# An FFN's output GEMM by seven block products for 16 of 22 f-tiles, its input GEMM in two passes, and the weight sums on GpSimd

## The chip, the cores and the metric

The kernel runs on one core of a Trainium2 chip. The metric is the device time of one execution in microseconds (us); lower is better. The engines are the tensor engine (PE, whose weight loads are shown as PEld), the vector engine (DVE), the scalar engine (ACT), GpSimd (POOL) and the sync engine (SP, which here only issues DMAs). Each works through its own queue in order, and semaphores hold them together.

## The reference

One encoder block on x of 1024 tokens by 1024 features in float32:

```python
def swiglu(x, w_in, w_out):
    gate, up = jnp.split(x @ w_in, 2, axis=-1)
    return (jax.nn.silu(gate) * up) @ w_out

x = x + 0.5 * swiglu(rmsnorm(x, ffn1_norm_g), ffn1_w_in, ffn1_w_out)   # D_FF = 2816
proj = rmsnorm(x, mix_norm_g) @ w_mix_in        # 8200 columns: mLSTM, spatial gating, gates
x = x + (sigmoid(g_m) * h_m + sigmoid(g_s) * h_s) @ w_mix_out
x = x + 0.5 * swiglu(rmsnorm(x, ffn2_norm_g), ffn2_w_in, ffn2_w_out)
return rmsnorm(x, final_norm_g)
```

The change touches the two FFNs only. Between them lies the mixing stage, which keeps its code.

## The kernel before

**Layout and precision.** Activations lie with features on the 128 partitions and 512 tokens (one of two token halves) in the free dimension. A float32 operand is used as a high part in float32r and the float32r remainder; a product of two operands is three matmuls (high-high, high-low, low-high: `PROD`). `unit` makes such a pair from a weight tile: a cast on ACT and a subtraction on DVE (L286, L287); `split` (L190, L191) does the same for an activation.

**Input GEMM.** w_in has 22 f-tiles of 128 gate columns and 22 of 128 up columns. For one f-tile, the features (two halves of 512), the tokens (two halves) and the pair gate/up form a 2 x 2 by 2 x 2 block product, and `group` computes it with seven block products in place of eight (the Winograd form of Strassen's scheme). Each product is 4 k tiles x 3 = 12 matmuls of 128 x 128 by 512 columns (`prod`, L293). The weight operands are sums and differences of the four raw blocks (`combine`, L299, on DVE); the activation operands, `B["t1"]` to `B["t4"]` and `B["22"]`, are made once by `operands`. Two of the seven products, with `B["11"]` and `B["21"]`, need only the first token half. For the first ten f-tiles (`EARLY`) `first_products` computes these two ahead of time, while the second token half is still being turned, and sends the results (`eb`) to DRAM; `group` fetches them back through POOL's DMA queue (L331, L333). For the other twelve f-tiles `group` does all seven. A group ends with the two h tiles of its f-tile, gate and up already multiplied and split. It is a generator: its first half ends at the `yield` of L346, its second after both h tiles.

**Output GEMM.** The f-tiles form blocks of three (the last has four, `BLOCKS`, L21). When a block's groups are done, its `down` is held back until the first half of the next block's first group has been issued. `down` takes w_out in four loads, and for each of eight output tiles and both token halves runs n x 3 matmuls (`down_mm`, L394), scales by 0.5 on ACT (L386) and adds into the residual in DRAM with an accumulating DMA from POOL (L387). The last block goes through `last`, which adds into the loaded residual (L421) and calls what follows.

**Buffers and order.** Raw weights have 3 buffers for the whole program (`rawp`), split weights 4 (`fw`), weight sums 3 (`fs`), h and early tiles 8 (`hp`), FFN temporaries 6 (`cp`, tag c) and general temporaries 4. Six PSUM banks serve the products. `bigp`, 16 tiles, holds `B["11"]`, `B["21"]`, `B["22"]` and `B["t4"]` during an FFN. The framework puts each engine's instructions in an order of its own; the program's order gives the priority. SP issues the weight loads, POOL the eb traffic and the accumulates.

Of the kernel before, what the change touches and what calls it, by code (L numbers as in the profile page):

```python
# [13 lines left out]
P = 128  # L14
# [6 lines left out]
BLOCKS = [(0, 3), (3, 3), (6, 3), (9, 3), (12, 3), (15, 3), (18, 4)]  # L21
EARLY = 10
SPAD = 40
MPAD = 24
HEADS = 4
# [8 lines left out]
def block_body(ctx, tc, x, ffn1_norm_g, ffn1_w_in, ffn1_w_out, mix_norm_g, w_mix_in, mlstm_conv_w,  # L34
# [8 lines left out]
    rawp = ctx.enter_context(tc.tile_pool(name="rawp", bufs=3))  # L43
    bigp = ctx.enter_context(tc.tile_pool(name="bigp", bufs=16))
    tps = []
    sp = ctx.enter_context(tc.tile_pool(name="sp", bufs=2))
# [14 lines left out]
    def open_temps(stack, n, bufs):  # L61
        tps.append(stack.enter_context(tc.tile_pool(name=f"tp{n}", bufs=bufs, reuse_waits="tile")))

    open_temps(f1, 1, 4)
# [53 lines left out]
    eb = [[[tc.dram_tile([P, NH], F32, name=f"eb{s}{f}{j}") for j in range(2)] for f in range(EARLY)]  # L118
          for s in range(2)]

    def load_unit(w_rows, ks, c0, extra=None):
        n = len(ks)
        nc_ = 2 * P if extra is None else 2 * P + extra[1]
        raw = rawp.tile([P, n, nc_], F32, tag="raw", name="raw")
# [138 lines left out]
    class Ffn:  # L263
        def __init__(self, stack, n, w_in, w_out):
            pool = lambda nm, b: stack.enter_context(tc.tile_pool(name=nm + n, bufs=b, reuse_waits="tile"))
            self.tx = pool("tx", 12)
            self.hp, self.wp, self.sp_ = pool("hp", 8), pool("fw", 4), pool("fs", 3)
            self.cp = pool("cp", 6)
            self.w_in, self.w_out = w_in, w_out
            self.B = {}  # L270
            self.eb = eb[int(n) - 1]

        def c512(self):
            return self.cp.tile([P, NH], F32, tag="c", name="c")

        def raw(self, f, d, both):
            r = rawp.tile([P, 4, 2, P], F32, tag="raw", name="raw")
# [12 lines left out]
        def prod(self, bank, w, b, start, stop):  # L290
            for i in range(4):
                for pi, (x, y) in enumerate(PROD):
                    PE.matmul(out=bank, lhsT=w[:, x, i, :], rhs=self.B[b][i][:, y, :],  # L293
                              start=(start and i == 0 and pi == 0), stop=(stop and i == 3 and pi == 2),
                              skip_group_check=True)

        def combine(self, a, b, op):
            s = self.sp_.tile([P, 4, P], F32, tag="s", name="s")
            V.tensor_tensor(out=s, in0=a, in1=b, op=op)  # L299
            return s  # L300

        def first_products(self, fs):
            st = []
            for f in fs:
                w = self.unit(self.raw(f, 0, False)[:, :, 0, :])
                a = bank("mm")
                self.prod(a, w, "11", True, False)
# [4 lines left out]
            for f, a, e in st:  # L312
                w = self.unit(self.raw(f, 1, False)[:, :, 0, :])
                self.prod(a, w, "21", False, True)
# [3 lines left out]
        def group(self, f):  # L318
# [3 lines left out]
            early = f < EARLY  # L322
            if not early:
                w = self.unit(a11)
                a = bank("mm")
                self.prod(a, w, "11", True, False)
                p1 = self.c512()
                A.copy(out=p1, in_=a)
            else:
                p1 = self.c512()  # L330
                G.dma_start(out=p1, in_=self.eb[f][0])  # L331
                sg1 = self.c512()
                G.dma_start(out=sg1, in_=self.eb[f][1])  # L333
            s1 = self.combine(a21, a22, ALU.add)
            s2 = self.combine(s1, a11, ALU.subtract)
            w = self.unit(s2)
# [4 lines left out]
            if not early:  # L341
                w = self.unit(a12)
                self.prod(a, w, "21", False, True)
                sg1 = self.c512()
                A.activation(out=sg1, in_=a, func=AF.Silu)
            yield  # L346
            s3 = self.combine(a11, a21, ALU.subtract)
            w = self.unit(s3)
            b = bank("mm")
            self.prod(b, w, "t3", True, True)  # L350
# [4 lines left out]
            self.prod(d, w, "t1", True, False)  # L355
# [652 lines left out]
```

## Time and profile before

| what | value |
|---|---|
| median of three runs | 2301.2 us (2300.08 to 2303.76) |
| the profiled execution | 2302.14 us, span 2300.0 us |
| PE busy | 2263.1 us (98%), 11171 matmuls |
| DVE busy | 1355.5 us (59%) |
| ACT busy | 992.9 us (43%) |
| POOL busy | 270.1 us (12%), nearly all of it issuing DMAs |
| DMA | 282.08 MB, mean 123 GB/s |

The stages by PE's timeline: the start and the first products of FFN1 to about 95 us, FFN1's groups and blocks to 699, the mixing stage to 1615, FFN2 to 2300. Busy is the share of time in which an engine executes; its idle time is put down to the instruction that released it last. Matmul ends are modelled, so the period of a run of matmuls is read from the starts of two neighbouring runs.

### The profile page before, as it was taken

The numbers are of one execution on the slowest core, as the hardware profiler recorded it, in microseconds if no ns is written. First come the engines' busy times: TensorE is split into PE (matmuls) and PEld (weight loads), VectorE is DVE, ScalarE is ACT, GpSimd is POOL, SyncE is SP. The second block draws the span as 40 slices with busy tenths as digits, with TensorE's granted clock in tenths as the row PEclk, the third lists the DMA queues.
The fourth block names the chain that finished last, engine by engine and source line by source line (L and its number), as shares of the span: only waits on it lengthen the run. The fifth ranks groups of instructions, "written<-read, shape, count | busy, mean of one in ns | idle before, by whom it ended". The sixth has DMA issues, their size and how long they took to land. (4 is left out here: it accounts for less than half of the span.)

```text
span 2300.0 us, 29669 instructions
## 1 busy us (share of the span) xinstructions
PE 2263.1 (98%) x11171; PEld 1908.0 (83%) x11171; DVE 1355.5 (59%) x2409; ACT 992.9 (43%) x1589; POOL 270.1 (12%) x394
## 2 busy tenths in 40 slices
PE   7999999999999999999999999999999999999998
PEld 5788888888888988888889888888778888888887
DVE  6845644634666658556646575565775446446466
ACT  5533333333345346445434554543633333333332
POOL 2221121021020000000000000000312220210200
PEclk9999999999999999999999999999999999999999
DMA  8775575274453234322353353324757772643633
GB/s 259 226 150 131 140 130 101 69 133 88 96 180 114 83 92 120 98 86 83 92 152 97 92 156 92 92 74 133 244 151 158 143 141 69 129 97 79 124 101 110
DMA packets 280367, 282.08 MB, mean 123 GB/s; under 512 B 16664, under 2 KB 236440, under 8 KB 280224
## 3 DMA queue, kind: packets, MB, share of 16 engines
q1 hardware_dynamic: 237600, 181.54, 26.7%
q0 software_dynamic: 42368, 98.59, 21.4%
q8 instruction: 87, 1.43, 0.3%
q14 instruction: 56, 0.46, 0.1%
q10 hardware_dynamic: 256, 0.07, 0.0%
HBM read 198.32 MB, written 81.82 MB: 122 GB/s over the span
## 5 line engine op out<-in xcount | busy, mean ns | idle before, releaser
L293 PE MATMUL mm<-b,fw 128*128 128x512 f32 x2640 | 609.4, 389 | 2.5 <-ACT b L190 1.6
L293 PEld LDWEIGHTS mm<-b,fw 128*128 128x128 f32 x2640 | 494.7, 188 | 108.0 <-ACT b L190 2.6
L157 PE MATMUL mm<-xn,w 128*128 128x512 f32 x2304 | 546.0, 391 | 0.0
L157 PEld LDWEIGHTS mm<-xn,w 128*128 128x128 f32 x2304 | 426.8, 188 | 82.8
L394 PE MATMUL mm<-h,fw 128*128 128x512 f32 x1728 | 393.6, 389 | 0.0
L394 PEld LDWEIGHTS mm<-h,fw 128*128 128x128 f32 x1728 | 324.3, 188 | 67.4
L287 DVE TENSOR_TENSOR fw<-raw,fw 128x512 fp32r<-128x512 f32 (+1 forms) x228 | 143.9, 632 | 228.2 <-ACT fw L286 227.2
L133 DVE TENSOR_TENSOR w<-raw,w 128x1024 fp32r<-128x1024 f32 (+2 forms) x146 | 176.4, 1209 | 144.4 <-ACT w L132 144.1
L293 PE MATMUL mm<-xn,fw 128*128 128x512 f32 x1056 | 254.4, 394 | 4.8 <-ACT xn L190 2.1
L387 POOL DMA_DIRECT2D xd<-c x192 | 165.9, 865 | 645.2 <-ACT c L386 632.4
L293 PEld LDWEIGHTS mm<-xn,fw 128*128 128x128 f32 x1056 | 199.0, 189 | 51.4 <-ACT xn L190 3.7
L132 ACT CAST w<-raw 128x1024 fp32r<-128x1024 f32 (+2 forms) x146 | 151.2, 1038 | 156.1 <-PE mm L157 82.1
L386 ACT ACTIVATE c<-mm 128x512 f32<-128x512 f32 x192 | 114.7, 597 | 237.0 <-PE mm L394 175.6
L287 DVE TENSOR_TENSOR fw<-s,fw 128x512 fp32r<-128x512 f32 x176 | 120.8, 688 | 127.4 <-ACT fw L286 126.6
L286 ACT CAST fw<-raw 128x512 fp32r<-128x512 f32 (+1 forms) x228 | 130.3, 573 | 150.5 <-PE mm L293 90.2
L171 PE MATMUL mm<-w,xn 128*128 128x256 f32 x1344 | 166.8, 285 | 0.2
L171 PEld LDWEIGHTS mm<-w,xn 128*128 128x128 f32 x1344 | 164.5, 193 | 1.8 <-DVE w L133 0.6
L286 ACT CAST fw<-s 128x512 fp32r<-128x512 f32 x176 | 108.4, 618 | 129.8 <-PE mm L293 116.1
L394 PE MATMUL mm<-h,wl 128*128 128x512 f32 (+1 forms) x480 | 95.6, 352 | 0.0
L190 ACT CAST h<-c 128x512 fp32r<-128x512 f32 x88 | 54.7, 622 | 91.8 <-DVE c L363 72.8
L157 PE MATMUL po<-mh,w 128*128 128x512 f32 x384 | 87.5, 389 | 0.0
L394 PEld LDWEIGHTS mm<-h,wl 128*128 128x128 f32 x480 | 77.7, 189 | 11.4 <-issue 0.5
(233 smaller groups left out, 2012.2 us busy)
## 6 DMA issues: line engine op xcount, KB each, us to landing
raw<-in_w_mix_in_dram SPq DMA_DIRECT2D x124, 512.0 KB, 3.7
raw<-in_ffn_w_in_dram SPq DMA_DIRECT2D x216, 256.0 KB, 4.5
xd<-c POOLq DMA_DIRECT2D x192, 256.0 KB, 5.4
raw<-in_ffn_w_out_dram SPq DMA_DIRECT2D x48, 384.0 KB, 3.0
eb<-early POOLq DMA_DIRECT2D x40, 256.0 KB, 3.9
c<-eb POOLq DMA_DIRECT2D x40, 256.0 KB, 3.1
xl<-xd POOLq DMA_DIRECT2D x32, 256.0 KB, 3.4
xr<-xd SPq DMA_DIRECT2D x32, 256.0 KB, 3.3
```

What stands on the lines that cost most here:

```text
L132: A.copy(out=w[:, 0, 0:n, :], in_=raw[:, 0:n, :])
L133: V.tensor_tensor(out=w[:, 1, 0:n, :], in0=raw[:, 0:n, :], in1=w[:, 0, 0:n, :].bitcast(F32), op=ALU.subtract)
L157: PE.matmul(out=banks[j], lhsT=w[:, a, i, j * P:(j + 1) * P], rhs=act[k][:, b, ts], start=(k == first and pi == 0), stop=(k == last and pi ...
L171: PE.matmul(out=o, lhsT=act[k][:, b, t * P:(t + 1) * P], rhs=w[:, a, i, :], start=(t % 2 == 0 and k == 0 and pi == 0), stop=(t % 2 == 1 an ...
L190: A.copy(out=dst[:, 0, :], in_=src)
L286: A.copy(out=w[:, 0], in_=src)
L287: V.tensor_tensor(out=w[:, 1], in0=src, in1=w[:, 0].bitcast(F32), op=ALU.subtract)
L293: PE.matmul(out=bank, lhsT=w[:, x, i, :], rhs=self.B[b][i][:, y, :], start=(start and i == 0 and pi == 0), stop=(stop and i == 3 and pi == 2),
L386: A.activation(out=xt, in_=o, func=AF.Copy, scale=0.5)
L387: G.dma_start(out=acc[t][d + j], in_=xt, accum_op=ALU.add)
L394: PE.matmul(out=o, lhsT=w[:, x, i, :], rhs=hs[i][:, y, ts], start=(i == 0 and pi == 0), stop=(i == n - 1 and pi == 2))
```

## The change

- `first_products` now runs for all 22 f-tiles, two at a time: the first ten as before between the `operands` calls, the other twelve after them. `eb` has 22 entries per FFN. `group` has only the five products with `t2`, `t3`, `t1`, `t4` and `22`, and fetches the `eb` tiles through SP's queue.
- The four weight sums of a group are made on POOL in place of DVE, and three of them overwrite raw blocks (`sums`).
- Blocks are now four of 4 f-tiles, one of 2 and the last of 4. For the 16 f-tiles of the first four blocks (`FAST`) the output GEMM uses the same seven-product scheme: pairs of f-tiles, pairs of output tiles (d and d + 4) and the token halves form the blocks. After each odd f-tile DVE makes four differences of h tiles, and seven h operands are split per pair in place of four. `down_fast` makes the sums of w_out on POOL, evicts with the factor 0.5 on ACT and DVE, and accumulates four tiles per output pair. f-tiles 16 to 21 keep `down` and `last`.
- Buffers: raw weights get a pool for each stage (4 buffers in the FFNs, 3 in the mixing stage); FFN temporaries join the general ones (11); h tiles go from 8 to 7, weight sums from 3 to 2; the h combinations lie in `bigp`. The load of the final gain moves to the first use.

```diff
-BLOCKS = [(0, 3), (3, 3), (6, 3), (9, 3), (12, 3), (15, 3), (18, 4)]
-EARLY = 10
+BLOCKS = [(0, 4), (4, 4), (8, 4), (12, 4), (16, 2), (18, 4)]
+FAST = 16
+TMP = 11
...
+        def sums(self, a11, a12, a21, a22, n):
+            s1 = self.sp_.tile([P, n, P], F32, tag="s", name="s")
+            G.tensor_tensor(out=s1, in0=a21, in1=a22, op=ALU.add)
+            G.tensor_tensor(out=a21, in0=a11, in1=a21, op=ALU.subtract)
+            G.tensor_tensor(out=a11, in0=s1, in1=a11, op=ALU.subtract)
+            return s1
...
         def group(self, f):
...
+            u2 = self.c512()
+            nc.sync.dma_start(out=u2, in_=self.eb[f][0])
+            s1 = self.sums(a11, a12, a21, a22, 4)
+            w = self.unit(a11)
             b = bank("mm")
-            self.prod(b, w, "t2", True, True)
-            u2 = self.c512()
-            V.tensor_tensor(out=u2, in0=b, in1=p1, op=ALU.add)
...
+            self.prod(b, w, self.B["t2"], True, True)
+            V.tensor_tensor(out=u2, in0=b, in1=u2, op=ALU.add)
+            w = self.unit(a21)
...
             c22 = self.c512()
             V.tensor_tensor(out=c22, in0=d, in1=u3, op=ALU.add)
+            yield
+            sg1 = self.c512()
+            nc.sync.dma_start(out=sg1, in_=self.eb[f][1])
...
+            G.tensor_tensor(out=a12, in0=a12, in1=a11, op=ALU.subtract)
+            w = self.unit(a12)
+            self.prod(d, w, self.B["22"], False, True)
...
+            if f >= FAST:
+                self.hs.append((self.part(self.hp, u3), self.part(bigp, c22)))
+            elif f % 2 == 0:
+                self.H["11"].append(self.part(self.hp, u3))
+                self.odd = u3, c22
+            else:
+                h11, h12 = self.odd
+                H = self.H
+                H["21"].append(self.part(self.hp, u3))
+                V.tensor_tensor(out=h11, in0=h12, in1=h11, op=ALU.subtract)
+                H["t1"].append(self.part(bigp, h11))
+                V.tensor_tensor(out=h12, in0=c22, in1=h12, op=ALU.subtract)
+                H["t3"].append(self.part(bigp, h12))
+                V.tensor_tensor(out=h11, in0=c22, in1=h11, op=ALU.subtract)
+                H["t2"].append(self.part(bigp, h11))
+                V.tensor_tensor(out=u3, in0=u3, in1=h11, op=ALU.subtract)
+                H["22"].append(self.part(self.hp, c22))
+                H["t4"].append(self.part(bigp, u3))
             yield
+        def down_fast(self, f0, H, acc):
+            for d in range(4):
+                r = raws[-1].tile([P, 4, 2, P], F32, tag="raw", name="raw")
+                for j in range(2):
+                    nc.sync.dma_start(out=r[:, :, j, :], in_=self.w_out[f0 * P:(f0 + 4) * P, (4 * j + d) * P:(4 * j + d + 1) * P]
+                                      .rearrange("(k p) c -> p k c", p=P))
+                rv = r.rearrange("p (i s) j c -> p i s j c", s=2)
+                a11, a12, a21, a22 = rv[:, :, 0, 0, :], rv[:, :, 1, 0, :], rv[:, :, 0, 1, :], rv[:, :, 1, 1, :]
+                def half(o, x, y):
+                    V.scalar_tensor_tensor(out=o, in0=x, scalar=0.5, in1=y, op0=ALU.mult, op1=ALU.add)
+                w = self.unit(a11, 2)
+                a = bank("mm")
+                self.prod(a, w, H["11"], True, False)
+                u2 = self.c512()
+                A.activation(out=u2, in_=a, func=AF.Copy, scale=0.5)
+                s1 = self.sums(a11, a12, a21, a22, 2)
+                w = self.unit(a12, 2)
+                self.prod(a, w, H["21"], False, True)
+                c11 = self.c512()
+                A.activation(out=c11, in_=a, func=AF.Copy, scale=0.5)
+                G.dma_start(out=acc[0][d], in_=c11, accum_op=ALU.add)
+                w = self.unit(a11, 2)
+                b = bank("mm")
+                self.prod(b, w, H["t2"], True, True)
+                half(u2, b, u2)
+                G.tensor_tensor(out=a12, in0=a12, in1=a11, op=ALU.subtract)
...
+                w = self.unit(s1, 2)
+                e = bank("mm")
+                self.prod(e, w, H["t1"], True, False)
...
+                w = self.unit(a12, 2)
+                self.prod(e, w, H["22"], False, True)
+                half(u2, e, u2)
+                G.dma_start(out=acc[1][d], in_=u2, accum_op=ALU.add)
...
+        for f in range(10, NF, 2):
+            ffn1.first_products((f, f + 1))
```

## Rows read from the trace of the kernel before

**Rows 1.** The page, part 1: busy us (share of the span) xinstructions of each engine.
```profile
PE 2263.1 (98%) x11171; PEld 1908.0 (83%) x11171; DVE 1355.5 (59%) x2409; ACT 992.9 (43%) x1589; POOL 270.1 (12%) x394
```

**Rows 2.** PE's waits: what waited for what, us in total, times, longest.
```profile
PE ml L106 <- DMA xtok<-in_x_dram: 6.7, 1, 6.7
...
PE mm L293 <- ACT early L309: 1.9, 2, 1.3
PE mm L293 <- ACT b L190: 1.6, 1, 1.6
...
PE mm L293 <- ACT fw L286: 0.8, 1, 0.8
PE mm L293 <- DVE fw L287: 0.7, 1, 0.7
...
PE ml L574 <- DVE t L567: 0.2, 1, 0.2
```

**Rows 3.** PE's timeline: start, length, group xcount [idle before <-releaser].
```profile
96.28 40.45 PE L293 MATMUL mm<-b,fw 128*128 128x512 f32 x172 [1.59 <-ACT b L190]
...
169.21 40.96 PE L293 MATMUL mm<-b,fw 128*128 128x512 f32 x180
210.01 32.80 PE L394 MATMUL mm<-h,fw 128*128 128x512 f32 x144
242.65 40.96 PE L293 MATMUL mm<-b,fw 128*128 128x512 f32 x180
...
1673.97 44.13 PE L293 MATMUL mm<-b,fw 128*128 128x512 f32 x192 [0.80 <-ACT fw L286]
```

**Rows 4.** Windows: length, busy us (x) of PE PEld DVE ACT POOL, PEclk, DMA, GB/s.
```profile
0.00:57.50 57.50, 41.03 (x161) 31.51 (x162) 37.02 (x105) 33.46 (x78) 16.79 (x39) 0.91 0.82 259
57.50:115.00 57.50, 54.50 (x247) 43.42 (x246) 50.15 (x81) 29.79 (x53) 15.67 (x29) 1.00 0.72 226
...
172.50:230.00 57.50, 57.50 (x256) 47.60 (x255) 33.41 (x54) 20.63 (x37) 10.75 (x15) 1.00 0.59 131
...
632.50:690.00 57.50, 57.50 (x256) 47.13 (x255) 39.42 (x68) 24.08 (x40) 14.80 (x28) 1.00 0.54 180
```

**Rows 5.** Groups by line and shape: busy us, mean ns | idle before <-releasers.
```profile
L387 POOL DMA_DIRECT2D xd<-c x192 | 165.9, 865 | 645.2 <-ACT c L386 632.4 <-ACT fw L286 8.1 <-issue 4.6
...
L286 ACT CAST fw<-s 128x512 fp32r<-128x512 f32 x176 | 108.4, 618 | 129.8 <-PE mm L293 116.1 <-DVE s L299 13.5
...
L286 ACT CAST fw<-raw 128x384 fp32r<-128x384 f32 x96 | 48.7, 508 | 36.4 <-PE mm L293 28.4 <-issue 8.0
...
L421 DVE SCALAR_TENSOR_TENSOR xl<-mm,xl 128x512 f32<-128x512 f32 x24 | 16.5, 688 | 8.8 <-PE mm L394 7.4 <-DMA xl<-xd 1.4
...
L309 ACT COPY early<-mm 128x512 f32<-128x512 f32 x20 | 11.7, 584 | 6.1 <-PE mm L293 5.9
...
L215 DVE TENSOR_TENSOR acc<-acc,t 128x256 f32<-128x256 f32 x14 | 5.8, 416 | 0.0
```

**Rows 6.** DVE's timeline, a stretch back to back in FFN1.
```profile
329.01 0.69 DVE L299 TENSOR_TENSOR s<-raw,s 128x512 f32<-128x512 f32 x1
329.62 0.68 DVE L371 TENSOR_TENSOR c<-c 128x512 f32<-128x512 f32 x1
330.22 0.68 DVE L299 TENSOR_TENSOR s<-raw 128x512 f32<-128x512 f32 x1
331.02 0.69 DVE L191 TENSOR_TENSOR h<-c,h 128x512 fp32r<-128x512 f32 x1
```

**Rows 7.** POOL: its timeline at the start, and its largest memset by line.
```profile
1.22 0.29 POOL masks.py:199 TENSOR_SCALAR_AFFINE_SELECT ident<-ident 128x128 f32<-128x128 f32 x1
...
L513 POOL MEMSET v<- 128x2064 f32 x1 | 1.8, 1819 | 0.1
```

**Rows 8.** DMA issues of the page: count, KB each, median us to landing.
```profile
raw<-in_ffn_w_in_dram SPq DMA_DIRECT2D x216, 256.0 KB, 4.5
```

More of the change, by code (lines that the diff above doesn't have):

```diff
@@ L117, in block_body @@
     xs_ = [[tc.dram_tile([P, NH], F32, name=f"xs{s}{d}") for d in range(KT)] for s in range(2)]
-    eb = [[[tc.dram_tile([P, NH], F32, name=f"eb{s}{f}{j}") for j in range(2)] for f in range(EARLY)]
+    eb = [[[tc.dram_tile([P, NH], F32, name=f"eb{s}{f}{j}") for j in range(2)] for f in range(NF)]
           for s in range(2)]
@@ L123, in load_unit @@
         nc_ = 2 * P if extra is None else 2 * P + extra[1]
-        raw = rawp.tile([P, n, nc_], F32, tag="raw", name="raw")
+        raw = raws[-1].tile([P, n, nc_], F32, tag="raw", name="raw")
         rs = slice(ks[0] * P, (ks[0] + n) * P)
@@ L290, in prod @@
         def prod(self, bank, w, b, start, stop):
-            for i in range(4):
+            for i, t in enumerate(b):
                 for pi, (x, y) in enumerate(PROD):
[L293 to L300, printed above, removed]
+                    PE.matmul(out=bank, lhsT=w[:, x, i, :], rhs=t[:, y, :], start=(start and i == 0 and pi == 0),
+                              stop=(stop and i == len(b) - 1 and pi == 2), skip_group_check=True)
+        def sums(self, a11, a12, a21, a22, n):
[4 more added lines that the diff above has]
+            return s1
         def first_products(self, fs):
@@ new lines, in group, with part @@
+            yield
+        def part(self, pool, src):
+            t = pool.tile([P, 2, NH], F32R, tag="h" if pool is self.hp else "big", name="h")
+            split(src, t)
+            return t
+        def down_fast(self, f0, H, acc):
+            for d in range(4):
+                r = raws[-1].tile([P, 4, 2, P], F32, tag="raw", name="raw")
+                for j in range(2):
[21 more added lines that the diff above has]
+                G.tensor_tensor(out=a12, in0=a12, in1=a11, op=ALU.subtract)
+                w = self.unit(a21, 2)
+                b = bank("mm")
+                self.prod(b, w, H["t3"], True, True)
+                u3 = self.c512()
+                half(u3, b, u2)
+                w = self.unit(s1, 2)
+                e = bank("mm")
+                self.prod(e, w, H["t1"], True, False)
+                c22 = self.c512()
+                half(c22, e, u3)
+                G.dma_start(out=acc[1][d + 4], in_=c22, accum_op=ALU.add)
+                w = self.unit(a22, 2)
+                b = bank("mm")
+                self.prod(b, w, H["t4"], True, True)
+                half(u3, b, u3)
+                G.dma_start(out=acc[0][d + 4], in_=u3, accum_op=ALU.add)
+                w = self.unit(a12, 2)
+                self.prod(e, w, H["22"], False, True)
+                half(u2, e, u2)
+                G.dma_start(out=acc[1][d], in_=u2, accum_op=ALU.add)
@@ L376, in down @@
         def down(self, f0, n, hs, acc):
             for d in range(0, KT, 2):
-                raw = rawp.tile([P, n, 2 * P], F32, tag="raw", name="raw")
+                raw = raws[-1].tile([P, n, 2 * P], F32, tag="raw", name="raw")
                 nc.sync.dma_start(out=raw, in_=self.w_out[f0 * P:(f0 + n) * P, d * P:(d + 2) * P]
@@ L400, in last @@
             for d in range(0, KT, 2):
-                raw = rawp.tile([P, n, 2 * P], F32, tag="raw", name="raw")
+                raw = raws[-1].tile([P, n, 2 * P], F32, tag="raw", name="raw")
                 nc.sync.dma_start(out=raw, in_=self.w_out[f0 * P:(f0 + n) * P, d * P:(d + 2) * P]
@@ L438, in run @@
                     spread()
-                hs, self.hs = self.hs, []
-                if bi < len(blocks) - 1:
-                    pend = (f0, n, hs, src)
+                hs = self.hs
+                if f0 < FAST:
+                    pend = lambda f0=f0, H=H: self.down_fast(f0, H, src)
+                elif bi < len(blocks) - 1:
+                    pend = lambda f0=f0, n=n, hs=hs: self.down(f0, n, hs, src)
                 else:
@@ L946, in block_body @@
             ffn2.operands(i, get2)
+        for f in range(10, NF, 2):
+            ffn2.first_products((f, f + 1))
         PARTS = (1, 2)
         sts = [[Stats(4 // p) for _ in range(p)] for p in PARTS]
-        fg = bigp.tile([P, D], F32, tag="big", name="fg")
-        nc.sync.dma_start(out=fg, in_=final_norm_g.partition_broadcast(P))
+        fgs = []
         ys = []
@@ L955, in fin2 @@
             n = 4 // PARTS[h]
+            if not fgs:
+                fgs.append(bigp.tile([P, D], F32, tag="big", name="fg"))
+                nc.sync.dma_start(out=fgs[0], in_=final_norm_g.partition_broadcast(P))
+            fg = fgs[0]
             sts[h][part].add(xt)
```

59 lines of the change are left out of this document (14 added, 45 removed).

## The prediction

> **What bounds the kernel now.** I read the page first for which engine is full, then the tensor engine's list of waits, then its timeline, and only then the other engines inside the two FFN stages. Part 1 of the page has the tensor engine (PE) at 98% and the vector engine (DVE) at 59% [rows 1]. The list of PE's waits, 16 lines from 6.7 to 0.2 us, adds up to under 30 us, nearly all of it at the start of the program and at the seams between stages; no line of it belongs to the FFNs' steady loop [rows 2]. The timeline says the same: inside FFN1 a stretch of 180 input-GEMM matmuls starts at 169.21 and the 144 output-GEMM matmuls behind it start at 210.01, so the period is 40.80 / 180 = 0.2267 us; the next stretch starts at 242.65, and 32.64 / 144 is 0.2267 again [rows 3]. PE is therefore fed without a gap, and a matmul that disappears is worth its 0.2267 us as long as the other engines keep up. DVE is busy 69% in one window in which PE shows no idle time; in the one where it reaches 87%, PE loses 3.0 of 57.5 us, though start-up waits fall there as well [rows 4].
>
> **What is removed: matmuls.** The input GEMM keeps its 84 per f-tile. The output GEMM of four f-tiles takes 48 x 4 = 192 matmuls today; the new `down_fast` takes 4 output pairs x 7 products x 2 (k tiles) x 3 (splits) = 168. With 24 fewer per block, four blocks, two FFNs, 192 go: 192 x 0.2267 = 43.5 us.
>
> **The first pass grows by 12 f-tiles per FFN.** The same 24 matmuls per f-tile only move forward. They run 5.44 us per f-tile, beside 2 casts of 0.62 and 2 evictions of 0.59 on ACT [rows 5], 2.4 us, and 2 splits on DVE. The transfers are two loads and two writes of 256 KB, 1.05 MB in 5.44 us, 193 GB/s; the first two windows moved 259 and 226 GB/s [rows 4]. A load lands in 4.5 us [rows 8] and its buffer is held about 1.3 us longer for cast and split; with four buffers that allows one unit per 1.5 us, and one per 2.72 us is needed. So nothing is added; if loads slowed to where four buffers no longer cover, each late unit would cost up to its landing time, 4.5 us. The longer pass also gives the turned operands time: the idle 1.59 before the first combined products in FFN1 and 0.80 in FFN2 [rows 3] should go, -2.4 us. Behind them nothing is late: the next combined product then needs its eb tile, written tens of us earlier.
>
> **SP and the buffers.** The eb reads (44 per FFN, 20 before) move from POOL's queue to SP's, into a pool of 11 shared temporaries. What stands behind an eb read that waits for a temporary is the next weight load. At most about eight are live (four of the current group, two held over from the even f-tile, the next read, one or two draining), and weights are loaded a buffer set ahead, so I cost it at nothing; without the spare temporaries one wait is one DVE backlog, a few us. Block traffic: 4.2 MB of w_in, 2.1 of eb, 2.1 of w_out, 4.2 of accumulates in 92.5 us, 136 GB/s, where the window 172.5 to 230 holds 131 [rows 4]. Accumulating writes fall from 96 to 80 per FFN. The weight pool per stage puts the fourth FFN2 buffer on memory that the mixing stage uses to its end: at worst one load late, about 2 us once. The moved load of the final gain is hidden by the last block.
>
> **What DVE and ACT get.** Back to back, DVE starts a 512-column operation every 0.605 us [rows 6]; a 256-column one shows 0.416 [rows 5], less the same overlap 0.33. A block of four f-tiles now gives DVE:
> groups: 20 weight splits, 28 evictions and products, 14 splits of h combinations (8 before), 8 new h differences: 70 x 0.605 = 42.4 us;
> `down_fast`: 20 evictions x 0.605 + 28 splits of 256 columns x 0.33 = 21.3 us.
> Together 63.7 us, beside 408 matmuls x 0.2267 = 92.5 us: 69%, the share at which PE still ran without a gap. ACT has 20 casts, 4 Silu, 14 h casts, 28 small casts of about 0.40 (by the casts of 384 and 512 columns [rows 5]) and 8 evictions: some 40 us of 92.5, hidden. The load is uneven. An even f-tile has 13 DVE operations (7.9 us), an odd one 22 (13.3 us), each beside 60 matmuls (13.6 us).
>
> **What POOL gets.** Per block 16 sums of 512 columns and 16 of 256. No row before shows a two-operand sum on POOL. The nearest are its memset of 2064 columns, 1.82 us (0.88 ns a column, no operand read), and the select of 128 columns, 0.29 us (2.27 ns, one operand read) [rows 7]. Per 512 columns that is 0.45 us from below and, if a second operand doubles the select, 2.32 from above; it could not be below nothing for POOL, which had none of it. I take the select's 1.16 us, the row nearest in kind (0.58 for 256): 27.8 us per block, plus 16 accumulate issues of 0.865 [rows 5], 13.8: 42 of 92.5 us. In time it is covered: the cast of a unit waits for PE to release one of four buffers ([rows 5]: 116.1 us of waiting for PE against 13.5 for the sums), so units stand about three products, 8.2 us, ahead, and four raw buffers let POOL start on the next f-tile a group earlier. DVE loses the 16 sums that stood on it per four f-tiles, already left out of the count above.
>
> **Where I expect a loss.** At the end of a block the h combinations hang on the last product: sum, Silu, product, two differences, a cast and a split before H["t2"] is usable, with the next group's three evictions and about four unit splits among them. That is roughly 1.2 + 0.6 + 1.2 + 0.6 + 0.6 + 7 x 0.605 = 8.4 us in DVE's order, plus what POOL adds. PE comes to it after three products of the next group and two of the block, 8.2 + 2.7 = 10.9 us. I put 1 us per block there, 8 us in all (0 if POOL costs DVE nothing, 27 by the first rival).
>
> **Sum.** 2300.0 (span) - 43.5 - 2.4 + 8 = 2262.1; the profiled execution took 2302.14, 2.1 us more than its span, so 2264. It lies 0.9 above the median of the runs, well inside what a measurement of this kernel can tell from no change, 0.2% or 4.6 us.
>
> **Rivals.**
> *First: POOL's sums and DVE's two-operand work exclude each other.* Of DVE's 63.7 us per block, 50 operations x 0.605 + 9.2 = 39.5 us read two SBUF operands. If each sum stops DVE for its 1.16 us, an odd f-tile needs 13.3 + 4.6 = 17.9 us against 13.6, an even one 12.5, `down_fast` 21.3 + 9.3 = 30.6 against 38.1. A block still fits (91.5 of 92.5), but the second odd f-tile ends 4.3 - 1.1 + 4.3 = 7.5 us late, and in `down_fast`, where products last 1.36 us, three units ahead cover only 4.1: 3.4 us per block, 27 in all, so 2302.1 - 45.9 + 27 = 2283. For it: DVE is nearly full in odd f-tiles. Against it: 24 us of the block's DVE work has one operand in PSUM, and DVE has gaps that a sum can use; today's POOL work reads no operands, so the trace can't decide.
> The Trainium skill, "SBUF — State Buffer", section "Who interferes with whom", says just this: a vector instruction with two SBUF inputs and a GpSimd instruction that reads SBUF hold one shared port, and the second waits until the first is done. By that rule the time is this rival's and not the forecast; no run here shows it yet.
>
> *Second, slower than before: the same exclusion with sums dearer than the select.* The place is the same, DVE; the point at which it decides is when a block's 63.7 us and its sums pass 92.5 + 45.9 / 8 = 98.2 us, that is 34.5 us for 24 sums' worth of 512 columns, 1.44 us each. Half-way between my value and the upper bound, 1.74 us, a block takes 105.5, 13 more than PE, 104 in all: 2302.1 - 45.9 + 104 = 2360. For it: two operands instead of one. Against it: the select's row holds a fixed part that a longer sum spreads.
>
> *Third: POOL's order.* If the sums of the next output pair stand behind the last accumulate of this one, then from its last product run eviction 0.69 [rows 5], issue 0.87, three sums 1.74, cast 0.40, split 0.42 = 4.1 us, and two products cover 2.7: 1.4 us, three times per block, 24 times: 33 us, 2289. Against it: DVE's order in the timeline is not the program's (the first sum of the next f-tile, at 330.22, stands before the last split of this one [rows 6]), so the order is planned by readiness.
>
> **Chances.** Forecast 0.60 (its own range 2254, no stall at all, to 2275); first rival 0.16, of which 0.14 ends clearly faster; third 0.07, of which 0.05; second 0.17, of which 0.14 is slower and 0.03 within 0.2%. Faster 0.60 + 0.14 + 0.05 = 0.79, the same 0.02 + 0.02 + 0.03 = 0.07, slower 0.14. The range 2252 to 2304 leaves out the 0.14; its low end is the sum without stalls less 2 us for the seams. The upper bound of a sum (2.32 us: 215 us lost) lies outside and is part of that 0.14.
>
> **What would show it.** Matmuls fall from 11171 to about 10979, with the period still 0.2267. Right: PE's waits in the blocks stay near 1 us each, DVE's splits stay at 0.69 us and POOL's sums near 1.2. First rival: splits with a mean well over 0.69 and PE waiting for DVE at the first products of `down_fast`. Second: POOL sums above 1.44 us and PE gaps in every odd f-tile. Third: PE waiting three times per block on a cast that waits for POOL. Waits of SP for temporaries, or PE idle in the long first pass, would show the steps that I cost at nothing wrong. A period other than 0.2267 would upset everything.

## The result and the profile after

The changed kernel is 0.9% slower: 2322.03 us (2321.28 to 2324.8, 4 runs) against 2301.59 (2300.08 to 2303.76), ratio 1.009, 95% interval 1.0073 to 1.0108. The forecast was 2264 with a range up to 2304. The profiled span went from 2300.0 to 2320.9.

Part 1 of the page of the changed kernel, which answers to [rows 1]:

```profile
PE 2237.9 (96%) x10979; PEld 1872.3 (81%) x10979; DVE 1547.3 (67%) x2649; ACT 999.9 (43%) x1684; POOL 606.0 (26%) x674
```

The 192 matmuls are gone, and PE's share fell too: it is no longer fed without a gap. Its waits (what waited for what, us in total, times, longest), where [rows 2] had no line of the FFNs' steady loop:

```profile
PE mm L294 <- DVE c L341: 17.8, 17, 2.1
PE mm L294 <- DVE c L391: 15.3, 8, 2.1
PE mm L294 <- DVE fw L288: 7.4, 9, 1.3
PE mm L294 <- ACT fw L287: 6.2, 5, 1.9
PE ml L239 <- DVE t L236: 2.7, 1, 2.7
```

PE's timeline over one block of four f-tiles of FFN1 (the `mm<-h` rows are `down_fast`, the `mm<-b` rows the groups):

```profile
317.70 1.97 PE L294 MATMUL mm<-h,fw 128*128 128x512 f32 x8
321.00 35.49 PE L294 MATMUL mm<-h,fw 128*128 128x512 f32 x154 [1.32 <-DVE fw L288]
358.58 1.63 PE L294 MATMUL mm<-h,fw 128*128 128x512 f32 x6 [2.09 <-DVE c L391]
360.05 16.50 PE L294 MATMUL mm<-b,fw 128*128 128x512 f32 x72
377.38 13.85 PE L294 MATMUL mm<-b,fw 128*128 128x512 f32 x60 [0.83 <-ACT fw L287]
392.91 13.85 PE L294 MATMUL mm<-b,fw 128*128 128x512 f32 x60 [1.68 <-DVE c L341]
407.08 11.16 PE L294 MATMUL mm<-b,fw 128*128 128x512 f32 x48 [0.32 <-DVE c L341]
418.07 1.97 PE L294 MATMUL mm<-h,fw 128*128 128x512 f32 x8
```

From 317.70 to 418.07 the block takes 100.4 us for 408 x 0.2267 = 92.5 us of matmuls. Three places lose: the start of `down_fast` (321.00), its last product (358.58), and the fifth product of a group (377.38, 392.91, 407.08). That fifth product adds into the bank which the eviction of the third product, L341, has to read first, and L341 is late in DVE's queue. Compare [rows 3], where such stretches follow each other without a wait.

At 377.38 the row names a cast, but the L341 that this product needs ends at the same moment, 377.24. It stood in DVE's queue behind a split, the split behind a cast, and the cast behind a sum (DVE, then ACT):

```profile
375.40 1.23 DVE L288 TENSOR_TENSOR fw<-raw,fw 128x512 fp32r<-128x512 f32 x1 [3.56 <-ACT fw L287]
376.56 0.68 DVE L341 TENSOR_TENSOR c<-mm,c 128x512 f32<-128x512 f32 x1
```

```profile
374.75 1.14 ACT L287 CAST fw<-raw 128x512 fp32r<-128x512 f32 x2 [5.06 <-POOL raw L302]
```

So a sum that comes late behind its load plays a part as well (POOL had waited 8.27 us for it, until 370.36). PE's wait of this kind is 0.83 us and stands in three of the eight blocks.

The whole account: from FFN1's first product to the mixing stage's first matmul 685.2 us (before 673.3), the mixing stage 915.0 (915.7), FFN2 694.9 (685.4): +11.9 - 0.7 + 9.5 = 20.7 of the 20.9. Removed matmuls and start gaps were to give 23 us in each FFN, so the two lost 35 and 32.

The other two engines, grouped by line and shape (busy us, mean ns | idle before). DVE:

```profile
L288 DVE TENSOR_TENSOR fw<-raw,fw 128x512 fp32r<-128x512 f32 x264 | 207.0, 785 | 145.0 <-ACT fw L287 142.6 <-PE mm L448 2.3
L288 DVE TENSOR_TENSOR fw<-raw,fw 128x256 fp32r<-128x256 f32 x208 | 118.8, 584 | 19.0 <-ACT fw L287 19.0
L349 DVE TENSOR_TENSOR c<-c 128x512 f32<-128x512 f32 x44 | 48.7, 1108 | 34.4 <-DMA c<-eb 34.2
L391 DVE SCALAR_TENSOR_TENSOR c<-mm,c 128x512 f32<-128x512 f32 x160 | 110.0, 687 | 61.1 <-PE mm L294 60.8
```

and POOL:

```profile
L302 POOL TENSOR_TENSOR raw<-s,raw 128x512 f32<-128x512 f32 x44 | 70.7, 1607 | 2.3
L300 POOL TENSOR_TENSOR s<-raw 128x512 f32<-128x512 f32 x44 | 68.0, 1546 | 223.6 <-DMA raw<-in_ffn_w_in_dram 203.9 <-DVE fw L288 11.8 <-DVE c L341 5.8
L408 POOL TENSOR_TENSOR raw<-raw 128x256 f32<-128x256 f32 x32 | 33.4, 1043 | 43.1 <-ACT fw L287 37.7 <-DVE fw L288 5.4
```

DVE operations with two SBUF operands are longer than they are without the sums (0.688, 0.418 and 0.689 us for the first three rows in e3, a run below); the one that reads PSUM (L391) is not. A 512-column sum takes 1.5 to 1.6 us, not the 1.16 that I took.

One collision close up, at the end of a `down_fast`, DVE first:

```profile
352.42 0.69 DVE L391 SCALAR_TENSOR_TENSOR c<-mm,c 128x512 f32<-128x512 f32 x1 [1.46 <-PE mm L294]
353.03 3.60 DVE L288 TENSOR_TENSOR fw<-raw,fw 128x256 fp32r<-128x256 f32 x2
356.56 0.68 DVE L391 SCALAR_TENSOR_TENSOR c<-mm,c 128x512 f32<-128x512 f32 x1
```

and POOL in the same stretch:

```profile
351.13 1.60 POOL L301 TENSOR_TENSOR raw<-raw 128x512 f32<-128x512 f32 x1
352.98 1.93 POOL L302 TENSOR_TENSOR raw<-s,raw 128x512 f32<-128x512 f32 x1
354.98 1.37 POOL L350 TENSOR_TENSOR raw<-raw 128x512 f32<-128x512 f32 x1
```

The two splits take 3.60 us where such a pair takes 0.75 elsewhere (at 343.42). The sum at L302 ends at 354.91, the one at L350 at 356.35, and DVE's pair at 356.63: it looks as if each split got through only when a whole sum was done. The evictions L391 behind them are late, and PE's wait of 2.09 at 358.58 is for the second of them, which ends at 358.44.

### The profile page after: what moved, and what is told of

Read it like the earlier page. It is cut to its first block, busy times and chain, and to the rows that moved or that the text cites. A ratio compares the mean times of both kernels' runs of the same rounds, so it can differ in the third digit from the quotient of the medians.

```text
span 2320.9 us, 30647 instructions
## 1 busy us (share of the span) xinstructions
PE 2237.9 (96%) x10979; PEld 1872.3 (81%) x10979; DVE 1547.3 (67%) x2649; ACT 999.9 (43%) x1684; POOL 606.0 (26%) x674
## 3 DMA queue, kind: packets, MB, share of 16 engines
q0 software_dynamic: 38400, 92.30, 18.7%
## 5 line engine op out<-in xcount | busy, mean ns | idle before, releaser
L288 DVE TENSOR_TENSOR fw<-raw,fw 128x512 fp32r<-128x512 f32 (+1 forms) x472 | 325.9, 696 | 164.0 <-ACT fw L287 161.7
L294 PE MATMUL mm<-h,fw 128*128 128x512 f32 x1344 | 313.4, 393 | 21.2 <-DVE c L391 15.3
L287 ACT CAST fw<-raw 128x512 fp32r<-128x512 f32 (+1 forms) x472 | 242.3, 524 | 207.4 <-PE mm L294 133.6
L294 PEld LDWEIGHTS mm<-h,fw 128*128 128x128 f32 x1344 | 249.0, 188 | 83.9 <-issue 12.6
L192 ACT CAST h<-c 128x512 fp32r<-128x512 f32 x136 | 82.8, 620 | 218.5 <-DVE c L349 152.1
L300 POOL TENSOR_TENSOR s<-raw 128x512 f32<-128x512 f32 (+1 forms) x76 | 95.5, 1257 | 287.1 <-DMA raw<-in_ffn_w_in_dram 203.9
L391 DVE SCALAR_TENSOR_TENSOR c<-mm,c 128x512 f32<-128x512 f32 x160 | 110.0, 687 | 61.1 <-PE mm L294 60.8
L193 DVE TENSOR_TENSOR h<-c,h 128x512 fp32r<-128x512 f32 x136 | 100.2, 756 | 32.0 <-ACT h L192 31.6
L302 POOL TENSOR_TENSOR raw<-s,raw 128x512 f32<-128x512 f32 (+1 forms) x76 | 94.3, 1240 | 51.2 <-DVE fw L288 48.9
L301 POOL TENSOR_TENSOR raw<-raw 128x512 f32<-128x512 f32 (+1 forms) x76 | 93.4, 1229 | 5.2
```

The lines of the kernel that those rows point to most:

```text
L193: V.tensor_tensor(out=dst[:, 1, :], in0=src, in1=dst[:, 0, :].bitcast(F32), op=ALU.subtract)
L287: A.copy(out=w[:, 0], in_=src)
L288: V.tensor_tensor(out=w[:, 1], in0=src, in1=w[:, 0].bitcast(F32), op=ALU.subtract)
L294: PE.matmul(out=bank, lhsT=w[:, x, i, :], rhs=t[:, y, :], start=(start and i == 0 and pi == 0), stop=(stop and i == len(b) - 1 and pi == 2 ...
L300: G.tensor_tensor(out=s1, in0=a21, in1=a22, op=ALU.add)
L302: G.tensor_tensor(out=a11, in0=s1, in1=a11, op=ALU.subtract)
```

## The experiments

Theories, by the letters that the expectations use. A: POOL's sums and DVE's operations with two SBUF operands hold each other up. B: DVE simply has too much of its own. C: the reads of `eb` and the weight loads, now in one SP queue, come late. D: the sums are late because they stand in a chain behind each load. E, formed on the way: where sums stand on DVE, its queue stands behind a sum that waits for its load. After each time, its ratio to the kernel before (run on the same chip) and the ratio's 95% interval stand in brackets; spans are those of the profiled executions.

**Is it the sums, and their reading?** Three edits of `sums` and of the fourth sum in the groups.

```
e1_sums_on_dve (all four sums alike)
-            G.tensor_tensor(out=s1, in0=a21, in1=a22, op=ALU.add)
+            V.tensor_tensor(out=s1, in0=a21, in1=a22, op=ALU.add)
e2_no_sums (all four gone, the units take plain weights)
-            G.tensor_tensor(out=s1, in0=a21, in1=a22, op=ALU.add)
-            return s1
+            return a21
e3_write_only_sums (a12 likewise)
+            for o in (s1, a21, a11):
+                for _ in range(3):
+                    G.memset(o, 0.03)
```

> The changed kernel with all its weight sums on DVE in place of POOL, nothing else moved. Theory A (POOL's sums and DVE's operations with two SBUF operands hold each other up): DVE gets 16 x 0.605 + 16 x 0.33 = 15 us more per block (78.7 of 92.5) but nothing beside it, so the 63 us that PE now loses in the blocks shrink by half or more: about 2285 us (2268 to 2300), splits back at 0.69 us. Theory B (DVE has too much work of its own after odd f-tiles, with or without POOL): 15 us more per block makes it worse, about 2340. Theory C (eb reads and weight loads in one SP queue come late): unchanged, about 2320.

> The changed kernel with the weight sums left out (the products use the raw blocks, so the output is not the reference's); DMAs, splits, evictions and matmuls stay. Theories A and D (D: the sums on POOL come late for their units, a matter of the chain behind each load) both say that nearly all of the 63 us goes: about 2262 us (2255 to 2275). Theory B: DVE has the same work, so 2300 or more. Theory C: the eb reads stay behind weight loads on SP, 2300 or more.

> Each weight sum on POOL is replaced by three memsets of its output tile (the sum is left out, so the output is not the reference's): POOL is held for about as long (3 x 0.45 us per 512 columns), the units wait for the same tiles, but POOL reads nothing from SBUF. Theory A, if reading is what collides: DVE's splits back at 0.69 us and the time near that without sums, about 2265 us. Theory D (late chain behind the load): no change, about 2320. Theory B and C: about 2320.

e1: 2351.16 (1.0224, 1.0209 to 1.024). e2: 2274.62 (0.9892, 0.9877 to 0.9907). e3: 2269.46 (0.9866, 0.9844 to 0.9888). In e1 DVE's splits are back at 0.688, as A expected, but the time is not: it is 66 us above A's 2285 and nearer to B's 2340; the reason comes below, with v1. Without sums the blocks are PE's alone (PE's timeline of e2; 213.91 to 306.74 is 92.8 us):

```profile
213.91 38.59 PE L294 MATMUL mm<-h,fw 128*128 128x512 f32 x168
252.34 54.56 PE L294 MATMUL mm<-b,fw 128*128 128x512 f32 x240
```

In e3 POOL is kept as busy with memsets, which write the same tiles and read nothing. POOL's group and DVE's splits of e3:

```profile
L302 POOL MEMSET raw<- 128x512 f32 x264 | 165.7, 699 | 67.6 <-DMA raw<-in_ffn_w_in_dram 62.1 <-issue 2.0 <-ACT fw L287 1.6
```

```profile
L288 DVE TENSOR_TENSOR fw<-raw,fw 128x512 fp32r<-128x512 f32 x264 | 181.5, 688 | 123.3 <-ACT fw L287 121.9 <-PE mm L294 0.7
L288 DVE TENSOR_TENSOR fw<-raw,fw 128x256 fp32r<-128x256 f32 x208 | 85.1, 418 | 37.7 <-ACT fw L287 37.7
```

Three memsets of 0.70 us take longer than a sum, and the units still wait for them: casts stand 32.5 us behind POOL, against 46.5 in the changed kernel. Yet the splits are back at 0.688 and the time is no longer than e2's. So it is not POOL's time, but that POOL reads SBUF beside DVE's second operand (A). The chain behind the load (D) is not quite the same in e3, as the memset of `s` waits for no load; what speaks against D as the main cause is w2 below, where the loads come earlier, the casts' wait for POOL halves to 22.9 us, and the time still rises. The Trainium skill, "SBUF — State Buffer", section "Who interferes with whom", says that a DVE instruction with two SBUF inputs contends with a GpSimd instruction that reads SBUF, not with one that only writes it, and that a DVE instruction with at most one SBUF input, outside the 2-port modes, does not contend. All three show here: 0.785 beside sums, 0.688 beside memsets, 0.687 for the eviction from PSUM.

What the sums cost is the difference of the spans, 2320.9 - 2272.8 = 48.1 us (46 by the ratios).

**Does a collision always reach PE?**

```
e6_before_pool_sums (the kernel before, its function combine)
-            V.tensor_tensor(out=s, in0=a, in1=b, op=op)
+            G.tensor_tensor(out=s, in0=a, in1=b, op=op)
e5_no_h_combinations (the four differences and three splits; t2 and t4 as t3)
-                V.tensor_tensor(out=h11, in0=h12, in1=h11, op=ALU.subtract)
+                H["t3"].append(H["t1"][-1])
x4_one_sum_twice (the line a second time)
+            G.tensor_tensor(out=s1, in0=a21, in1=a22, op=ALU.add)
```

> The kernel before with nothing changed but the engine of its weight sums: POOL in place of DVE. Theory A says that the collision costs PE only where DVE is short of time: here DVE has about 60% and PE's units stand three products ahead, so splits get longer (0.75 or more in the mean) but PE loses little: 2300 to 2310. If sums on POOL are late in themselves: 2330 or more.

> The changed kernel (sums on GpSimd) without the combinations of h: per pair of f-tiles four differences and three splits on DVE and their casts are left out, and the output GEMM's combined products read one plain operand instead, so the output is not the reference's. Matmuls, GpSimd's sums and all transfers stay. If the collision costs PE time only where DVE is short of time, the odd f-tiles, 3 x 0.75 + 4 x 1.0 = 6.3 us of DVE work lighter, keep up: the groups come to 13.6 us per f-tile, and what is left is the loss inside the down stretch (42.3 against 38.1 us); 2322 - 8 x (7.4 - 4.2) = 2296 us, within 6. If instead each collision reaches PE wherever it happens, the blocks stay at 99 us or more and the time within 2316 to 2322.

> The changed kernel with the first sum of every unit set issued twice on GpSimd (the second writes the same values): 76 more sums to the 304. If the price goes with the number of sums, 47 us / 304 = 0.157 us each, the time rises by 12 us to 2334, within 5. If it goes with which DVE work they meet, the sums behind the doubled one come 1.3 to 1.6 us later and the time can fall on either side, by up to 25 us as five buffers did.

e6: 2314.95 (1.0061, 1.0046 to 1.0076); its steady blocks keep the old times although DVE's operations are longer there too (512-column splits 0.793 at L287, against 0.688 in the kernel before; PE's timeline of e6, to be read beside [rows 3]):

```profile
176.71 40.96 PE L293 MATMUL mm<-b,fw 128*128 128x512 f32 x180
217.51 32.80 PE L394 MATMUL mm<-h,fw 128*128 128x512 f32 x144
```

Its 14 us, which put it above the 2300 to 2310 expected by A, fall at the FFNs' start, for two reasons. In FFN1 PE waits 4.83 us at 98.57 behind a DVE that is busy without a break and longer at its work (two operations of L892 take 2.86 us at 92.13, where such a pair takes 1.5 in the kernel before): a collision in the stretch in which the turned operands load DVE most ([rows 4]). But DVE's wait of 4.77 at 104.00 is for a read that POOL issued only after a row of sums, and in FFN2 PE waits 5.50 us at 1685.26 for an ACT copy that stood behind a cast, which waited 4.98 for sums of 1.26 and 1.27 us behind a late load. So e6 shows that the steady blocks pay nothing; at the start, collisions and late sums were not told apart. e5: 2297.91 (0.9992, 0.9983 to 1.0001), within 2 us of what was expected where DVE's slack decides. x4: 2350.58 (1.0207, 1.019 to 1.0224). The 304 sums cost 48.1 / 304 = 0.16 us each, the 76 added ones 28.6 / 76 = 0.38: the price of a collision is what DVE has no slack for, and it seems to grow as the slack goes. x4's second sum also lengthens the chain behind each load (casts wait 63.0 us for POOL, not 46.5), and part of its rise is PE's clock (108 matmuls behind a gap of 1.97 take 26.39 us, not 24.8), so the 0.38 is not all collision. B is half right: DVE's own load is no loss by itself (e2, 92.8 us per block), but it sets what a collision costs.

**Shorter sums, fewer sums.**

```
v4_sums_in_pieces (all four sums alike)
-            G.tensor_tensor(out=s1, in0=a21, in1=a22, op=ALU.add)
+            for i in range(n):
+                G.tensor_tensor(out=s1[:, i], in0=a21[:, i], in1=a22[:, i], op=ALU.add)
v2_down_sums_on_dve (down_fast's sums on DVE)
+            E = V if n == 2 else G
+            E.tensor_tensor(out=s1, in0=a21, in1=a22, op=ALU.add)
```

> The changed kernel, each weight sum on POOL cut into instructions of 128 columns (4 per 512, 2 per 256); the same sums, 256 more instructions per FFN and more. Theory A (a sum on POOL and a DVE operation with two SBUF operands exclude each other for a whole instruction): a DVE split now waits at most for a piece of about 0.4 us instead of 1.3, so splits get shorter (below 0.785 us in the mean for 512 columns) and the 3 us holds of one split at the end of down_fast go: 2280 to 2300. If instead the two share the port's rate, the total of delay stays and the time with it, about 2322 or more, since POOL has more instructions.

> The changed kernel with down_fast's sums (256 columns) on DVE, the groups' sums (512) on POOL. Theory A: down_fast has DVE at 21.3 + 5.3 = 26.6 of 38.1 us and its small splits fall from 0.584 to about 0.45 us, so PE's losses there shrink; the collisions of the 512-column sums stay: about 2310. Theory E (what cost the version with all sums on DVE was a DVE queue standing behind sums that wait for late weight loads): the loads of w_out come early enough in down_fast, so no new wait: also about 2310, and not above 2325.

v4: 2325.25 (1.0126, 1.0093 to 1.0158), no gain: 512-column splits average 0.794 (0.785 in the changed kernel), 256-column ones 0.543 (0.584), so shorter holds do not help. A's 2280 to 2300 was wrong; the other forecast, 2322 or more if the two share a rate, came. Whether the holds are shorter but more, or are shared, v4 does not tell. v2: 2315.12 (1.0062, 1.0047 to 1.0077): 7 us better than the change, the 256-column splits at 0.512, the 512-column ones still at 0.783.

**Late loads.**

```
e4_eb_on_pool (sg1 likewise)
-            nc.sync.dma_start(out=u2, in_=self.eb[f][0])
+            G.dma_start(out=u2, in_=self.eb[f][0])
v1_sums_on_dve_5raw (e1, and)
-TMP = 11
+TMP = 9
-bufs=3 if n == 2 else 4
+bufs=3 if n == 2 else 5
```

> The eb reads go back to POOL's queue as in the kernel before, all else as changed. Theory C: DVE's 34 us of waiting for eb tiles go and the weight loads move up, about 2295 us. Theories A, B and D: within 5 us of 2322, or a few us slower, as 88 more issues of 0.55 us stand between the sums on POOL.

> All weight sums on DVE, raw weights 5 buffers instead of 4, temporaries 9 instead of 11. Theory E (with the sums on DVE its queue stood 140 us behind weight loads): the loads come a buffer earlier, the 5 us stall per block shrinks or goes: 2300 or less, against 2351 with 4 buffers. If DVE's load alone made it slow (79 of 92.5 us per block): still above 2340.

e4: 2339.92 (1.0188, 1.0152 to 1.0224), where C expected 2295; the reads then stand behind POOL's sums, so moving them is no remedy there. v1: 2302.43 (1.0006, 0.9997 to 1.0015), 49 us better than e1 by one weight buffer (and two temporaries fewer). The same group, DVE's first sum, of e1:

```profile
L300 DVE TENSOR_TENSOR s<-raw 128x512 f32<-128x512 f32 x44 | 30.4, 691 | 140.0 <-DMA raw<-in_ffn_w_in_dram 140.0
```

and of v1:

```profile
L300 DVE TENSOR_TENSOR s<-raw 128x512 f32<-128x512 f32 x44 | 30.4, 691 | 78.5 <-DMA raw<-in_ffn_w_in_dram 74.9 <-issue 3.3
```

In e1 DVE stood 140 us behind first sums whose weights had not landed, with evictions queued behind them (E); v1's blocks take 94.5 us instead of 102.2 (the means of three in FFN1).

**The same buffer with sums on POOL.** This should have helped as well, or done nothing.

```
w2_pool_sums_5raw (the changed kernel) and x2_no_h_comb_5raw (e5)
-TMP = 11
+TMP = 9
-bufs=3 if n == 2 else 4
+bufs=3 if n == 2 else 5
x1_nine_temporaries (the changed kernel)
-TMP = 11
+TMP = 9
```

> The changed kernel (sums on GpSimd) with five weight buffers instead of four and nine temporaries instead of eleven; nothing else. If the 25 us per FFN that its blocks lose are the port alone (A), the weights' lateness does not matter: splits stay at 0.785 us, blocks at 99.5 to 100.4 us, and the time is 2322 within 5 us. If part of the loss is sums that start late behind their loads (D), a fifth buffer gives GpSimd its operands one f-tile earlier: PE's wait for the cast of a combined unit in the groups (0.83 and 1.9 us) goes, DVE's splits stay slow, and the time falls to between 2300 and 2312.

> The changed kernel with nine temporaries instead of eleven and its four weight buffers. If the 34 us of the run with five buffers and nine temporaries came from the temporaries (reads of eb that wait for one hold up the weight queue), this takes 2350 us or more. If it came from the fifth buffer, which lets GpSimd's sums start earlier and fall on the h combinations, this takes 2322 us within 5.

> Five weight buffers and nine temporaries with sums on GpSimd, without the combinations of h (four differences and three splits of DVE per pair of f-tiles left out, output not the reference's). If the fifth buffer hurts because the sums meet the h combinations at DVE's fullest place, it no longer hurts here: 2298 us, as with four buffers, within 8. If it hurts whatever DVE does there, the 34 us stay: 2325 to 2335.

w2: 2355.9 (1.0244, 1.0229 to 1.026), 34 us worse, which neither theory expected: D expected 2300 to 2312 from earlier loads, A no change. x1: 2325.36 (1.0097, 1.0082 to 1.0112): nine temporaries alone are not it, so the fifth buffer is. x2: 2317.72 (1.0069, 1.0054 to 1.0084), 20 us above e5, where 0 or 27 and more were expected: taken as a difference of differences, the h combinations account for 34 - 20 = 14 of the 34. DVE's h differences in the changed kernel:

```profile
L367 DVE TENSOR_TENSOR c<-c 128x512 f32<-128x512 f32 x16 | 11.1, 692 | 0.5
L369 DVE TENSOR_TENSOR c<-c 128x512 f32<-128x512 f32 x16 | 11.0, 685 | 0.0
```

and in w2:

```profile
L369 DVE TENSOR_TENSOR c<-c 128x512 f32<-128x512 f32 x16 | 19.7, 1231 | 0.0
L367 DVE TENSOR_TENSOR c<-c 128x512 f32<-128x512 f32 x16 | 18.9, 1180 | 0.5
```

With four buffers the sums of two f-tiles happen to run before the odd f-tile's differences; with five the sums of the next f-tile run beside them. Another part is PE's clock. PE's timeline of w2, from the odd f-tile on:

```profile
281.30 15.45 PE L294 MATMUL mm<-b,fw 128*128 128x512 f32 x60 [2.47 <-DVE c L341]
300.24 27.23 PE L294 MATMUL mm<-b,fw 128*128 128x512 f32 x108 [3.48 <-DVE c L341]
```

and windows of the same stretch (length, busy us (x) of the engines, then the granted clock):

```profile
297.00:300.20 3.20, 0.00 (x0) 0.00 (x0) 3.20 (x7) 1.18 (x3) 0.00 (x0) 0.77 0.30 90
300.20:304.00 3.80, 3.76 (x9) 3.02 (x10) 2.59 (x4) 0.00 (x0) 1.46 (x2) 0.50 1.00 316
304.00:310.00 6.00, 6.00 (x24) 4.86 (x24) 4.94 (x9) 3.02 (x5) 0.00 (x0) 0.87 0.05 14
310.00:318.00 8.00, 8.00 (x37) 6.61 (x36) 4.62 (x8) 1.86 (x3) 0.00 (x0) 1.00 0.58 169
```

PE was idle for 3.48 us; in the next 3.8 us the granted clock is 0.50 (its 1.2 GHz level), and the 108 matmuls take 27.23 us where they take 24.8 at full clock (x1, v2). The 60 after the gap of 2.47 take 15.45; in the changed kernel the 60 after the gap of 1.68 at 392.91 take 13.85, with the clock at 1.00. The length of a gap alone does not decide: the changed kernel has a gap of 2.09 (358.58) after which the clock reads 1.00, and one of 2.13 after which it reads 0.64 for 3.8 us, so that 132 matmuls take 31.36 us, not 30.1:

```profile
258.24 2.01 PE L294 MATMUL mm<-h,fw 128*128 128x512 f32 x6 [2.13 <-DVE c L391]
260.05 31.36 PE L294 MATMUL mm<-b,fw 128*128 128x512 f32 x132
```

So 4.0 us of the loss of 13 us in w2's block is clock, on top of gaps of 1.84 + 2.47 + 3.48. How much of x2's 20 us is clock and how much more collisions I did not separate.

**A version that beats both.**

```
w1_five_fast_blocks (v1, and)
+BLOCKS = [(0, 4), (4, 4), (8, 4), (12, 4), (16, 4), (20, 2)]
+FAST = 20
w3_five_fast_6raw (w1, and)
+TMP = 7
+bufs=3 if n == 2 else 6
w4_five_fast_eb_on_pool (w1, and; sg1 likewise)
+            G.dma_start(out=u2, in_=self.eb[f][0])
```

> A variant meant to beat both: all sums on DVE, five weight buffers and nine temporaries (2302 us as it stands), and the seven products for 20 of the 22 f-tiles: blocks of 4, 4, 4, 4, 4 and a last one of 2. 24 matmuls less per FFN, 48 x 0.2267 = 10.9 us, and the plain block of two, at whose end PE waited 7.7 us per FFN for a split behind late loads, is gone. If that stall came from the plain block's loads in the queue (E), the time is 2302 - 10.9 - 15 = 2276, within 8 us. If DVE's backlog only moves on to the last block (B), the stall comes back there and the time is 2288 to 2296.

> As the variant with seven products for 20 of 22 f-tiles and all sums on DVE, with a sixth weight buffer taken from the temporaries (seven instead of nine). If DVE's queue still stands behind sums that wait for their loads (75 us of such waiting with five buffers, 140 with four; E), a sixth buffer takes the blocks from 94.3 to the 92.8 us of PE's work: 8 us less than with five buffers. If seven temporaries are too few, the reads of eb wait on the weight queue for a free one, and the time is 5 to 20 us above.

> The version with seven products for 20 of 22 f-tiles and all sums on DVE (2292 us), with the reads of eb on GpSimd's queue, which has only the accumulates now. If eb reads on the weight queue hold up weights in the blocks (C), blocks fall from 93.5 towards 92.8 us and the time to 2284 to 2289. If the rest is DVE's own load in the odd f-tiles (B; 26 operations, 15.7 us, beside 13.6 of PE), nothing changes: 2290 to 2295.

w1: 2291.83 (0.9967, 0.9955 to 0.9979). w3: 2292.33 (0.9964, 0.9953 to 0.9976), the same. w4: 2300.79 (0.9998, 0.9987 to 1.0009), worse, which neither C nor B expected. w1 is 8 us faster than the kernel before and 30 faster than the changed one. It misses E's 2276 by 16 and lies in the 2288 to 2296 that stood for B, but B's reason, that the wait comes back inside the block, does not show: the wait of 7.7 us in front of the last block is gone, and the block has no such wait. What is lost lies behind the blocks. The last block is shorter by 96 matmuls, 21.8 us, but the stretch from its start to the next stage shrinks only from 51.4 us (v1) to 36.6 in FFN1, and from 65.7 to 50.9 at the program's end, 7 us short each time. It seems that the shorter block no longer covers the norm behind it, as PE waits there (PE's timeline of w1, end of FFN1):

```profile
679.22 2.07 PE L239 MATMUL ml<-t,ones 128*128 128x512 f32 x2 [3.19 <-DVE t L236]
680.30 2.98 PE L448 MATMUL mm<-h,wl 128*128 128x512 f32 x6
690.90 3.86 PE L186 MATMUL mm<-w,xn 128*128 128x264 f32 x16 [7.62 <-ACT xn L192]
```

## Why the prediction was wrong

**Matmuls and period: right.** 10979 of them, and a stretch without a wait still runs at 0.2267 (e2: 168 in 38.59, the last one's drain included). The gain of 43.5 us is real.

**First pass and start gaps: right.** In the changed kernel the 288 matmuls from 87.90 on take 65.5 us without a wait, and the combined products start behind them at once.

**The failed step is "Where I expect a loss": 1 us per block, 8 in all.** It was 48.1 us for the sums (e2). I had counted DVE's operations at the lengths that they have beside a POOL that reads nothing; beside 304 sums the splits alone are 264 x 0.097 + 208 x 0.166 = 60 us longer, and L349 another 44 x 0.42 = 18 us. 69% of DVE's time was not the share to look at: the odd f-tile had 13.3 of 13.6 us by my own count, and a delay there can go on to PE. The cover that I gave the sums (units three products ahead) was too good as well: casts stood 46.5 us behind L302, where [rows 5] had 13.5 behind sums on DVE.

**The first two rivals had the mechanism, and the sign lay with the second.** The first gave 27 us and 2283 (chance 0.16) with 1.16 us per sum, from the select of [rows 7]; a sum takes 1.28 while DVE is idle (POOL at 373.44), and 1.5 to 1.6 in the mean of a group. Its own sign, splits well over 0.69 and PE waiting for DVE at `down_fast`, is what the profile shows. The second (chance 0.17) decided from 1.44 us per sum on, and the sums passed that. With 1.55 in its sum a block takes 63.7 + 24 x 1.55 = 100.9 us, so 2302.1 - 45.9 + 8 x 8.4 = 2323; the block took 100.4. That closeness is partly chance: DVE is not full over the block (233.5 us of 300 between 220 and 520, waiting for the port included), and by e2 the sums are 48 us of the loss, not 67. I had left the time of a sum, the term that decides between three outcomes, at one row of another operation with one operand.

**"I cost it at nothing" failed for SP's queue as well.** 18.7 us of e2's span are above 2300.0 - 45.9 = 2254.1, though it has no sums. About 12 of it are at f-tile 18, where the stretch from the last fast block's end to the last block takes 102.0 us in FFN1 and 100.6 in FFN2 for 95.2 of PE. DVE in e2 there:

```profile
593.13 0.69 DVE L345 TENSOR_TENSOR c<-c 128x512 f32<-128x512 f32 x1 [9.08 <-DMA c<-eb]
```

The `eb` read stands behind eight weight loads on SP (they begin at 559.27, it at 579.61), and DVE behind the read. The order alone does not decide: e3 has the same one (561.69 and 582.62), and that stretch takes 96.5 and 96.9 us there; in the changed kernel it takes 101.9 and 99.6. Another 4 are at the end of FFN1 (waits of 2.49 for DVE's t L236, none in the kernel before) and some 4 to 5 between the mixing stage and FFN2 (in the changed kernel 2.32 for DVE's acc L217 and 1.81 for ACT's fw L287); what makes these two late was not tried. e2's first product starts 1.7 us earlier than that of the kernel before, which goes the other way.

**The third rival** (POOL's order) did not come: between the output pairs PE runs 154 matmuls without a wait.

## What to carry to other kernels

Before work moves to GpSimd, count on DVE the operations with two SBUF operands in the tightest stretch, not over the span: there a sum that reads SBUF can hold one of them up by about its whole length (3.60 us for two splits, not 0.75). An operation with one operand in PSUM is not held up (0.687), and where DVE has slack the longer operations cost PE nothing (e6's blocks). A gap of PE costs itself and, where the rows show the granted clock falling behind it, the slower matmuls too. An engine that stands in order behind an operand that has not landed blocks all that is queued on it, so work that moves to a fuller engine may need its loads earlier (v1: one buffer, 49 us).

## What the runs showed of the hardware

A GpSimd sum of 512 fp32 columns with two SBUF operands takes 1.28 us while DVE is idle and one of 256 columns 0.74. In the changed kernel the means of the groups are 1.51 to 1.61 and 0.74 to 1.04. Cutting it into pieces of 128 columns (0.43 each at the shortest, 0.71 to 0.85 in the mean) brought no time (v4). Earlier loads made the kernel 34 us slower (w2): the sums moved beside DVE's fullest stretch, which by x2 is 14 of the 34, and PE's clock fell behind longer gaps; the rest was not separated.
